# A hand-written engine order through the RG-LRU rounds, with a two-phase long convolution as filler

## The chip, the cores and the metric

The kernel runs on one core of a Trainium2 chip. A core has five engines, each with its own in-order instruction queue: TensorE (PE in the profile) multiplies matrices and writes to PSUM, VectorE (DVE) and ScalarE (ACT) read and write both memories, GpSimd (POOL) works on SBUF alone, and SyncE (SP) issues most of the transfers. [...]

The metric is the device time of one execution in microseconds. Three runs of the kernel before gave 1373.71, 1376.23 and 1376.35 us; the median is 1376.23 us.

## What is computed

Two layers over a latent stream `x` of 1024 tokens with 1024 channels, with 256 context tokens beside it. The even layer is where the change lies (shapes for one sample, float32 throughout):

```python
z = h @ p["w_in"]                              # h: modulated rmsnorm of x
va, vg, ga, xb, gb = split(z)                  # 1024 channels each
u   = va * sigmoid(vg)                         # branch A
u   = depthwise_conv(u, conv_w, conv_b)        # 31 taps
y_a = silu(layernorm(u)) * silu(ga)
u   = depthwise_conv(xb, sconv_w, sconv_b)     # branch B: 4 taps
r, i = sigmoid(u @ w_r + b_r), sigmoid(u @ w_i + b_i)     # per head of 128, both directions
a   = exp(-8 * r * softplus(-lam))
bx  = sqrt(1 - a*a) * (i * u)
y_b = scan_forward(a, bx) + scan_backward(a, bx)          # started from the state after the context
y_b = y_b * silu(gb)
x   = x + gate * (concat([y_a, y_b]) @ p["w_out"])
```

The odd layer (a pooling mixer with two large products) and a last RMSNorm follow; nothing in them is changed.

## The kernel before

Tokens lie along the free dimension, channels along the 128 partitions, so each 1024-channel tensor is eight tiles of 128x1024. Products are made in three passes of a float32 split into a high and a low part (`mm3_steps`, lines 121 to 129: high x high, high x low, low x high), which is 24 matmuls of 512 columns for half a tile. A weight tile is loaded into a ring of two raw tiles (`wr`), its high part is cast on ScalarE into a ring of two (`wh`) and its low part is subtracted on POOL into a ring of two (`wl`); `wload` and `split` do this (lines 94 to 118).

The stages that matter here, with the names by which the profile shows them:

- Start: modulation, RMSNorm, and the first two of four weight foldings (to line 428). It leaves `hh`, `hl` (the latent stream in two parts) and `ch`, `cl` (the context).
- Recurrence (lines 430 to 586), a round for each tile `j`. The projections of a round are xb (latent tokens, into the two-bank PSUM tile `xb`) and xbc (context), vg and va, and four gates `g` (two directions, two gates each, in pieces of 256, 512 and 512 columns). The short convolution makes `uc` (first tap on ScalarE, line 531; three on VectorE, line 534), which is split into `uh` and `ul` for the gates' products. `u = va * sigmoid(vg)` (line 564) is the input of branch A. Of the previous tile, ScalarE makes tanh, exp and root (`decays`), POOL two products for each direction (lines 463 and 465), VectorE a combination and two scans for each direction (lines 468, 475, 477) and the sum of the directions (line 480), which goes to HBM (`yb_raw`).
- gb (lines 717 to 730): for each tile the projection gb, its SiLU, the product with `yb_raw` (read back as `yr`), and the split into `ybh`, `ybl`.
- The long convolution (lines 734 to 768): for each tile one start on ScalarE and 30 taps of about 1013 columns on VectorE, accumulating in the two-bank PSUM tile `conv`; sums over tiles for the mean go to `lnsum`, on POOL for tiles 1 to 5. It depends on `u` alone, so the scheduler spreads it over the recurrence, gb and wob stages.
- LayerNorm (lines 771 to 785): the mean by a product with a matrix of equal entries (`mu`), 16 subtractions (line 776), squares on ScalarE (lines 778, 781), their sums on VectorE for the first half of the tokens and on POOL for the second (line 783), a product `ms_ln`, a root and a reciprocal for each half; then 16 products (line 823) and a SiLU for each tile (line 824).
- wob (lines 788 to 798): the product of branch B's half of `w_out` with `ybh`, `ybl`; VectorE adds it to `x` out of PSUM (line 796).
- ga (lines 830 to 853): the projection ga, its SiLU in place in PSUM, the product with `u` (line 838), and the splits for the next product.

Matmul outputs of one bank come from a ring of four PSUM banks (`pm`); two further tiles of two banks each (`cv`, `xb`) serve the convolution and the projection xb. Two tile rings of SBUF hold the recurrence's tiles (`ltile`, six of 128x1280; `utile`, four), and four half tiles (`ttile`) serve the sigmoids.

The order on each engine is set by the scheduler of the framework, which places instructions by an estimated timeline and by the priority of the program order; `tc.high_priority` moves an instruction ahead, and `tc.issue_after` places one behind another. Once compiled, the order is fixed. In the recurrence of the kernel before, `issue_after` ties only ScalarE's decays to one another and a few instructions to them. Of the gate weights it says

```python
gws = wload(gw[j], f"gw{j}", nc.gpsimd, n=4 * P)
weave(gate_steps(j, gws, (uh, ul), gates), steps, 2)
```

so their high and low parts take a place in the rings `wh` and `wl` among xb, vg and va.

## Time and profile before

| | |
|---|---|
| median of the runs shown | 1376.23 us |
| the profiled execution itself | 1381.07 us |
| its span, first to last instruction | 1379.3 us |
| TensorE busy, mean granted clock | 1295.9 us (94%), 0.974 |
| VectorE busy | 1205.1 us (87%) |
| ScalarE, POOL busy | 632.7 us (46%), 363.3 us (26%) |
| recurrence, first vg matmul to first gb matmul | 104.3 to 476.4 us |
| gb, wob, ga | to 570.3, 663.4, 750.7 us |

A row of a view by stages has the stage, its length, and for PE, the weight load, DVE, ACT and POOL the busy time with the number of instructions in brackets; then the granted clock of TensorE (1.00 is full), the share of the transfer engines and GB/s. A row of a timeline has the start, the duration of the row's instructions (xN of them together), engine, line, operation and operands; in square brackets the idle time ahead of it and who ended it. A group's row has the count, busy time and mean in ns of one, and the idle time. A row of a tile's view has the shortest, median and longest duration in ns. The execution profiled is a single one, so times read from it are compared with its own 1381.07 us.

### The profile page before, as it was taken

The page shows a single profiled execution, that of the slowest core. Times are in us where ns is not written, and L with a number is a line of the kernel's source. Part 1 is how long each engine was busy: PE and PEld are TensorE (multiplying, and loading weights), DVE is VectorE, ACT ScalarE, POOL GpSimd, SP SyncE. Part 2 cuts the span into 40 slices and gives each one's busy share as a digit, 9 for nine tenths or more (in the row PEclk, how much of TensorE's full clock was granted, in tenths as well). Part 3 has the DMA queues.
Part 4 walks back from the last instruction along what each step waited for, and adds up shares of the span by engine and source line. Part 5 has one row for each costly group of instructions (what it writes and reads, how often), then busy time and mean ns, then how long its engine had stood idle before and what let it go on. Part 6 is the DMA issues. An engine that isn't in the chain of part 4 may idle for free.

```text
span 1379.3 us, 15637 instructions
## 1 busy us (share of the span) xinstructions
PE 1295.9 (94%) x5664; PEld 1048.2 (76%) x5664; DVE 1205.1 (87%) x1587; ACT 632.7 (46%) x906; POOL 363.3 (26%) x182
## 2 busy tenths in 40 slices
PE   7889989898999799999998999999999999999896
PEld 4468868787777587787887887788888888778685
DVE  7998999999999999998778865999999987876775
ACT  6353644674465542304533544754334344634442
POOL 5173534743473555523320004000000000000002
PEclk9899999999999899999999999999999999999997
DMA  9753011111112113343353646424243334758623
GB/s 354 280 180 119 25 59 54 53 40 61 54 35 72 46 46 130 110 151 135 103 185 122 221 154 205 138 93 151 100 145 123 115 115 132 265 190 275 206 107 123
DMA packets 82866, 181.79 MB, mean 132 GB/s; under 512 B 7778, under 2 KB 27618, under 8 KB 82788
## 3 DMA queue, kind: packets, MB, share of 16 engines
q1 hardware_dynamic: 74340, 176.60, 37.8%
q10 hardware_dynamic: 8448, 4.20, 1.0%
q8 instruction: 44, 0.72, 0.2%
q14 instruction: 34, 0.28, 0.1%
HBM read 136.72 MB, written 44.04 MB: 131 GB/s over the span
## 4 chain that ended last, share of the span: by engine, by line
PE 36%; DVE 10%; DMA 7%; issue 2%; ACT 2%; POOL 1%; POOLq 0%; SPq 0%; DVEq 0%; ACTq 0%
PE ga L127 2%; PE ga L128 2%; PE ga L126 2%; PE wob L127 2%; PE wob L128 2%; PE wob L126 2%; DMA wr_g<-wg 1%; DVE ws L986 1%; DMA yr_t<-y_t 1%; DMA wr_v<-wfold 1%; PE qb_g L666 1%; DVE wq_g L96 1%; PE qb_g L669 1%; PE qb_g L668 1%; DVE wq_wo L96 1%
## 5 line engine op out<-in xcount | busy, mean ns | idle before, releaser
L746 DVE SCALAR_TENSOR_TENSOR conv<-u,sm,conv 128x1013 f32<-128x1013 f32 (+14 forms) x232 | 291.2, 1272 | 6.6 <-ACT conv L738 3.8
L1252 POOL TENSOR_TENSOR o<-x,rr 128x256 f32<-128x256 f32 (+1 forms) x9 | 8.0, 923 | 462.9 <-ACT rr L1240 460.0
L511 ACT ACTIVATE g<-g,sm 128x512 f32<-128x512 f32 (+1 forms) x96 | 58.8, 617 | 110.5 <-PE g L510 108.3
L96 POOL TENSOR_TENSOR wl_wu<-wr_wu,wh_wu 128x1024 fp32r<-128x1024 f32 x16 | 39.4, 2470 | 153.9 <-ACT wh_wu L95 147.7
L463 POOL TENSOR_TENSOR g<-g,uc 128x1280 f32<-128x1280 f32 x16 | 47.5, 2967 | 107.9 <-ACT g L511 65.1
L249 PE MATMUL fold<-gh,wh_wu 128*128 128x512 f32 x128 | 53.0, 416 | 5.7 <-ACT wh_wu L95 5.7
L250 PE MATMUL fold<-gl,wh_wu 128*128 128x512 f32 x128 | 52.4, 409 | 3.2 <-DVE gl L96 3.2
L128 PE MATMUL gb<-h0h,wl_gb 128*128 128x512 f32 x128 | 50.7, 398 | 4.8 <-POOL wl_gb L96 4.8
L126 PE MATMUL vg<-h0h,wh_vg 128*128 128x512 f32 x128 | 52.3, 408 | 2.7 <-ACT g L511 2.1
L251 PE MATMUL fold<-gh,wl_wu 128*128 128x512 f32 x128 | 50.7, 405 | 2.3 <-POOL wl_wu L96 2.3
L128 PE MATMUL xb<-h0h,wl_xb 128*128 128x512 f32 x128 | 50.2, 392 | 2.0 <-POOL wl_xb L96 2.0
L127 PE MATMUL wob<-ybl,wh_wob 128*128 128x512 f32 x128 | 50.5, 395 | 1.2 <-POOL ybl L96 1.2
L465 POOL TENSOR_TENSOR g<-g,th 128x1280 f32<-128x1280 f32 x16 | 46.9, 2948 | 16.8 <-ACT th L449 16.8
L127 PE MATMUL vg<-h0l,wh_vg 128*128 128x512 f32 x128 | 51.2, 400 | 0.0
L126 PE MATMUL gb<-h0h,wh_gb 128*128 128x512 f32 x128 | 50.6, 395 | 0.1
L126 PE MATMUL va<-h0h,wh_va 128*128 128x512 f32 x128 | 50.6, 395 | 0.0
L127 PE MATMUL va<-h0l,wh_va 128*128 128x512 f32 x128 | 50.6, 395 | 0.0
L508 PE MATMUL g<-uh,wh_gw 128*128 128x512 f32 (+1 forms) x96 | 36.3, 379 | 15.1 <-ACT wh_gw L95 6.4
L126 PE MATMUL wob<-ybh,wh_wob 128*128 128x512 f32 x128 | 50.6, 396 | 0.0
L128 PE MATMUL wob<-ybh,wl_wob 128*128 128x512 f32 x128 | 49.9, 391 | 0.7 <-POOL wl_wob L96 0.7
L128 PE MATMUL va<-h0h,wl_va 128*128 128x512 f32 x128 | 50.4, 395 | 0.0
L127 PE MATMUL gb<-h0l,wh_gb 128*128 128x512 f32 x128 | 50.4, 393 | 0.0
(548 smaller groups left out, 4301.1 us busy)
## 6 DMA issues: line engine op xcount, KB each, us to landing
mod<-modT SPq DMA_DIRECT2D x28, 512.0 KB, 5.5
wr_wu<-wu SPq DMA_DIRECT2D x16, 512.0 KB, 3.9
x_part<-xp SPq DMA_DIRECT2D x32, 256.0 KB, 2.4
mod<-modT SPq DMA_DIRECT2D x32, 256.0 KB, 3.3
wr_v<-wfold SPq DMA_DIRECT2D x16, 512.0 KB, 3.7
wr_g<-wg SPq DMA_DIRECT2D x16, 512.0 KB, 5.4
wr_wo<-wo SPq DMA_DIRECT2D x16, 512.0 KB, 4.2
yr_t<-y_t SPq DMA_DIRECT2D x16, 512.0 KB, 6.3
```

The lines of the kernel that those rows point to most:

```text
L96: eng.tensor_tensor(out=lo, in0=src, in1=hi.bitcast(F32), op=sub))
L126: nc.tensor.matmul(ps, hi[:, kc], xh[k][:, cols], start=(k == 0), stop=False)
L127: nc.tensor.matmul(ps, hi[:, kc], xl[k][:, cols], start=False, stop=False)
L128: nc.tensor.matmul(ps, lo[:, kc], xh[k][:, cols], start=False, stop=(k == ks - 1))
L249: nc.tensor.matmul(ps, wh[:, kc], gh[i], start=(i == 0), stop=False)
L250: nc.tensor.matmul(ps, wh[:, kc], gl[i], start=False, stop=False)
L251: nc.tensor.matmul(ps, wl[:, kc], gh[i], start=False, stop=(i == 3))
L463: nc.gpsimd.tensor_tensor(out=ius[d], in0=ius[d], in1=uc, op=mult)
L465: nc.gpsimd.tensor_tensor(out=ius[d], in0=ius[d], in1=roots[d], op=mult)
L508: nc.tensor.matmul(ps[:, :n], gwh[:, kc], uh[:, a : a + n], start=True, stop=False)
L511: nc.scalar.activation(t[:, a : a + n], ps[:, :n], AF.Sigmoid, bias=col(ob + d * KT + j))
L746: nc.vector.scalar_tensor_tensor(out=(us[j] if k == 30 else acp)[:, a:b], in0=us[j][:, a + o : b + o], scalar=col(O_CONVW + 31 * j + k), i ...
```

## The change

Three things are changed, all in the even layer, and what is computed stays the same.

1. From the recurrence to the end of gb, every instruction of TensorE, VectorE, ScalarE and POOL is placed behind the one written ahead of it (`on`, with one last instruction for each engine), so each engine's order is that of the program text. A round is written out anew: its projections, the previous tile's tanh, exp, root, scans, and the casts and low parts of the weights, loaded by `raw_load` and split by `raw_split`. xbc and its taps now come ahead of xb; xb of the next tile is woven into the gates, 16 steps of three matmuls over 12 gate pieces. In the last round gb0 takes xb's place. gb runs two tiles ahead of the product with `yb_raw`, and the weights of the first two wob tiles are cast there too. Six fixed tiles `L` replace the ring `ltile`, and the modulation's tiles for the gate go through them ahead of round 0.
2. The long convolution works on even and odd tokens apart (`conv`): two convolutions of 15 and 16 taps on the halves with every second tap, one of 16 on the sum of the halves with summed weights (`wsum`, the last weight alone), and recombinations. Its instructions have some 508 columns and read every second element of `u`; both accumulators lie in the one PSUM tile. Each instruction is a step, and `fill(n)` takes the next n steps at a fixed place in VectorE's order: 32 in a round, 22 behind the last round, 6 for each half tile of gb. What is left at the end of gb (62 of 414 steps) is placed by the scheduler as before. All `lnsum` additions are on VectorE.
3. The gate weights' high and low parts move from the weights' rings to the half tiles of `tpool`.

```diff
+    def on(eng, f, *args, **kw):
+        with ExitStack() as octx:
+            if eng in last:
+                octx.enter_context(tc.issue_after(last[eng].ins))
+            last[eng] = f(*args, **kw)
+        return last[eng]
...
+    def raw_split(raw, name):
+        hi = wpool.tile([P, D], F32R, tag="wh", name=f"wh_{name}")
+        lo = wpool.tile([P, D], F32R, tag="wl", name=f"wl_{name}")
+        cast(hi, raw)
+        gp(out=lo, in0=raw, in1=hi.bitcast(F32), op=sub)
+        return hi, lo
...
+    def tap(acc_, src, w, o, last_=False):
+        a, b = max(0, -o), H - max(0, o)
+        vec(nc.vector.scalar_tensor_tensor, out=(src if last_ else acc_)[:, a:b], in0=src[:, a + o : b + o],
+            scalar=w, in1=acc_[:, a:b], op0=mult, op1=add)
+        if last_:
+            vec(nc.vector.tensor_copy, out=src[:, b:], in_=acc_[:, b:])
+
+    def conv(j, n):
+        acp = wide(f"conv{j}", n)
+        ue, uo = us[j][:, 0::2], us[j][:, 1::2]
+        acc_, late, bias = acp[:, HALF[0]], acp[:, HALF[1]], col(O_CONVB + j)
...
+        for n in range(NT + 1):
+            if n < NT - 1 and n != 7:
+                tap(acc_, ue, w(2 * n + 1), n - 7)
+                yield
+            if n != 8:
+                tap(late, uo, w(2 * n), n - 8)
+                yield
...
+        vec(nc.vector.tensor_tensor, out=uo, in0=uo, in1=ue, op=add)
+        yield
...
+        for n in range(NT + 1):
+            if n != 7:
+                tap(acc_, uo, wsum[:, j, n : n + 1] if n < NT else w(30), n - 7, n == NT)
+                yield
...
         for j in range(KT):
+            vg = [psum(f"vg{j}_{h}") for h in range(2)]
+            all_of(mm3_fixed(vg[0], w, (hh, hl), HALF[0]))
+            if state is not None:
+                rec_input(state, 1)
+            fill(2)
+            first_tap(j, xb, uc[:, C:])
+            other_taps(j, xb, uc[:, C:], 1)
+            if state is not None:
+                rec_tanh(state)
+            wva = raw_split(raw_load(win[j], f"va{j}"), f"va{j}")
+            if state is not None:
+                rec_exp(state)
             uh, ul = utile(f"uh{j}", F32R), utile(f"ul{j}", F32R)
+            cast(uh, uc)
+            all_of(mm3_fixed(vg[1], w, (hh, hl), HALF[1]))
+            fill(4)
+            vec(nc.vector.tensor_tensor, out=ul, in0=uc, in1=uh.bitcast(F32), op=sub)
+            if state is not None:
+                rec_root(state)
+                rec_scaled(state, 0)
+            name = "gb0" if final else f"xb{j + 1}"
+            wnext = raw_split(raw_load(win[4 * KT] if final else win[3 * KT + j + 1], name), name)
+            gwh, gwl = [tpool.tile([P, H], F32R, tag="t", name=f"w{n}_gw{j}") for n in "hl"]
+            raw = wpool.tile([P, H], F32, tag="wr", name=f"wr_gw{j}")
+            nc.sync.dma_start(raw, gw[j])
+            cast(gwh, raw)
+            gp(out=gwl, in0=raw, in1=gwh.bitcast(F32), op=sub)
+            if state is not None:
+                rec_scaled(state, 1)
...
+            for h in range(2):
+                ps = psum(f"va{j}_{h}")
+                all_of(mm3_fixed(ps, wva, (hh, hl), HALF[h]))
+                fill((8, 5)[h])
+                vec(nc.vector.tensor_tensor, out=u[:, HALF[h]], in0=ps, in1=sg[h], op=mult)
...
+            if state is not None:
+                rec_scan(state, 0)
+            if not final:
+                other_taps(j + 1, xc, ucn[:, :C])
+            if state is not None:
+                rec_scan(state, 1)
+                rec_sum(state)
...
+            for n, _ in enumerate(gate_steps(j, (gwh, gwl), (uh, ul), gates)):
+                while done < 16 * (n + 1) // 12:
+                    next(steps)
+                    done += 1
+                if n == 5:
+                    rec_input(now, 0)
+                if n == 6:
+                    w = raw_split(raw, name)
+            all_of(steps)
+            fill(10)
...
     for j in range(KT):
+        if j > 0:
+            sbs[j] = [ttile(f"sb{j}_{h}") for h in range(2)]
+            for h in range(2):
+                act(sbs[j][h], gps[j][h], AF.Silu)
+        if j + 2 < KT:
+            gps[j + 2] = [psum(f"gb{j + 2}_{h}") for h in range(2)]
+            for h in range(2):
+                all_of(mm3_fixed(gps[j + 2][h], gws[j + 2], (hh, hl), HALF[h]))
         th, tl = d2tile(f"ybh{j}", F32R), d2tile(f"ybl{j}", F32R)
         for h in range(2):
             y = vtile(f"yr{j}_{h}")
             nc.sync.dma_start(y, yb_raw[j][:, HALF[h]])
+            vec(nc.vector.tensor_tensor, out=y, in0=y, in1=sbs[j][h], op=mult)
+            cast(th[:, HALF[h]], y)
+            gp(out=tl[:, HALF[h]], in0=y, in1=th[:, HALF[h]].bitcast(F32), op=sub)
+            fill(6)
+        gb_weights(j + 3)
...
+    fixed[0] = False
+    all_of(going[0])
+    for j in range(begun[0], KT, 2):
+        all_of(zip(*[conv(k, n) for n, k in enumerate(range(j, min(j + 2, KT)))]))
```

329 lines of the change are left out of this document (177 added, 152 removed).

## The prediction

> **What bounds the kernel now.** I read the busy times of the page first, then the busy times by stage (recurrence, gb, wob, ga, cut at their first matmuls), then the groups of VectorE, then single stretches of the timeline.
>
> ```profile
> span 1379.3 us, 15637 instructions
> PE 1295.9 (94%) x5664; PEld 1048.2 (76%) x5664; DVE 1205.1 (87%) x1587; ACT 632.7 (46%) x906; POOL 363.3 (26%) x182
> ...
> 104.30:476.40 372.10, 345.40 (x1586) 284.15 (x1584) 353.49 (x297) 203.26 (x238) 176.38 (x69) 0.96 0.16 54
> 476.40:570.30 93.90, 89.12 (x384) 73.02 (x385) 92.28 (x77) 38.12 (x48) 54.23 (x29) 0.98 0.29 96
> 570.30:663.40 93.10, 91.25 (x393) 73.40 (x392) 86.69 (x94) 23.21 (x32) 34.43 (x19) 1.00 0.42 142
> 663.40:750.70 87.30, 87.30 (x385) 72.15 (x384) 67.11 (x145) 35.72 (x49) 17.26 (x7) 1.00 0.45 146
> ...
> 465.27 0.28 PE L508 MATMUL g<-uh,wh_gw 128*128 128x256 f32 x1
> 465.39 0.28 PE L509 MATMUL g<-ul,wh_gw 128*128 128x256 f32 x1
> ```
>
> The ga stage is TensorE at its pace: 385 matmuls in 87.30 us, 0.227 us each; 256 columns take 0.12 (465.27 to 465.39). By these the recurrence needs 7 rounds of 168 x 0.227 + 36 x 0.12 = 42.4 us, a last one of 28.7 and 2.9 for the first xbc: 328.4 of its 372.1 us. gb needs 87.1 of 93.9, wob 87.1 of 93.1. So 56.5 us are TensorE's idle or slow time. VectorE is busy 95% of the recurrence and 98% of gb: it sets both stages.
>
> ```profile
> L468 DVE SCALAR_TENSOR_TENSOR g<-g,g 128x1280 f32<-128x1280 f32 x16 | 42.4, 2650 | 5.9 <-POOL g L465 5.9
> ...
> L468 DVE SCALAR_TENSOR_TENSOR g<-g,g x16: 1458/2511/4243, 164.6 to 499.4; 128x1280 f32<-128x1280 f32 x16
> L475 DVE TENSOR_TENSOR_SCAN g<-g,g x16: 657/680/2875, 169.9 to 507.1; 128x256 f32<-128x256 f32 x16
> L477 DVE TENSOR_TENSOR_SCAN g<-g,g x16: 2320/2336/4480, 176.6 to 512.3; 128x1024 f32<-128x1024 f32 x16
> ...
> 259.55 3.85 DVE L468 SCALAR_TENSOR_TENSOR g<-g,g 128x1280 f32<-128x1280 f32 x1
> ...
> 259.09 2.96 POOL L465 TENSOR_TENSOR g<-g,th 128x1280 f32<-128x1280 f32 x1
> ```
>
> The first row gives a mean of 2.65 us for an instruction whose shortest is 1.458: 42.4 - 16 x 1.458 = 19 us, 2.4 a round, are lost in this line alone, and the two scans below it also reach 2.9 and 4.5 us at their longest. The pair at 259 shows the occasion: the drawn-out one of 3.85 us starts inside an instruction of POOL. All of them have two inputs in SBUF. The taps (one input in PSUM) show none of this.
>
> **The change part by part.** *Long convolution.* What a VectorE instruction costs in a queue is the step to the next one, not its duration, since neighbours overlap by some 0.08 us:
>
> ```profile
> 584.26 0.74 DVE L796 SCALAR_TENSOR_TENSOR xp<-wob,m,xp 128x512 f32<-128x512 f32 x1
> 584.93 4.81 DVE L746 SCALAR_TENSOR_TENSOR conv<-u,sm,conv 128x1015 f32<-128x1015 f32 x4
> 589.65 0.74 DVE L796 SCALAR_TENSOR_TENSOR xp<-wob,m,xp 128x512 f32<-128x512 f32 x1
> ```
>
> Four full taps take 589.65 - 584.93 = 4.72 us, 1.18 each; a 512-column instruction with a PSUM operand takes 584.93 - 584.26 = 0.667. Before, a channel tile is 30 x 1.18 = 35.4 us. After, it is 49 PSUM instructions of about 508 columns (2 starts, 28 + 1 taps, 2 recombinations, 15 taps, 1 finish), 49 x 0.667 = 32.7, and some 1.2 us of small ones and one sum: 33.9. That is 12 us less over eight tiles; lnsum additions moved from POOL to VectorE (ten of 0.6 us) give 6 back. The two phases alone are worth 6 us of VectorE, nothing on TensorE. All of this takes a read of every second word as free, which no row shows: a half-tap lies between 0.667 (the 512-column row) and 1.18 us (as if all words between were read). I take 0.667, the row with the same count of elements.
>
> *The order of a round.* Let T be the end of xb on TensorE. Rows for the round:
>
> ```profile
> 243.26 1.20 ACT L531 ACTIVATE uc<-xb,sm 128x1024 f32<-128x1024 f32 x1
> 244.70 2.62 ACT L449 ACTIVATE th<-g,chalf 128x1280 f32<-128x1280 f32 x2
> 247.78 1.05 ACT L95 CAST wh_va<-wr_va 128x1024 fp32r<-128x1024 f32 x1
> 249.44 1.28 ACT L449 ACT_TABLE_LOAD   x1
> 258.59 0.60 ACT L552 ACTIVATE sg<-vg 128x512 f32<-128x512 f32 x1
> 291.71 1.20 ACT L531 ACTIVATE uc<-xb,sm 128x1024 f32<-128x1024 f32 x1
> ...
> 272.97 0.68 DVE L564 TENSOR_TENSOR u<-va,sg 128x512 f32<-128x512 f32 x1
> 273.57 1.48 DVE L571 TENSOR_TENSOR ul<-uc,uh 128x1280 fp32r<-128x1280 f32 x1
> 248.29 1.28 DVE L534 SCALAR_TENSOR_TENSOR uc<-xb,sm,uc 128x1022 f32<-128x1022 f32 x1
> 287.26 0.48 DVE L534 SCALAR_TENSOR_TENSOR uc<-xbc,sm,uc 128x255 f32<-128x255 f32 x1
> 280.75 1.21 DVE L480 TENSOR_TENSOR g<-g,g 128x1024 f32<-128x1024 f32 x1
> ...
> 286.04 2.96 POOL L463 TENSOR_TENSOR g<-g,uc 128x1280 f32<-128x1280 f32 x1 [13.04 <-PE g L510]
> 291.31 2.40 POOL L96 TENSOR_TENSOR wl_vg<-wr_vg,wh_vg 128x1024 fp32r<-128x1024 f32 x1 [2.30 <-ACT wh_vg L95]
> ```
>
> Before, a round is 291.71 - 243.26 = 48.45 us (from one first tap on xb to the next). After, VectorE has in a round: 32 conv steps 21.3, three long and three short taps 4.8, ul 1.4, two u 1.2, two scan groups of 4.2, a sum 1.1: 38.2 us, and waits 1.4 for the first tap behind T. That fits in TensorE's 42.4. Now the timetable by these rows, each engine in its written order, all times behind T. VectorE's taps and fills end at 9.6. ScalarE (first tap, tanh, va cast, load, exp, uh cast, load) has uh at 10.2, the first root at 12.8, sg at 17.6 and 18.1. VectorE goes on with ul (11.6), eight fills (16.9), u0 (18.3), u1 (22.6, since va's second half ends at 21.8), scans (26.8), ctx taps (28.0), scans (32.2), sum (33.4), ten fills (40.1) and two of the next round. POOL ends its first input at 2.3, va lo 7.4, scaled input 15.8, xb lo 18.2, gate lo 19.5, second scaled input 22.5, and begins the next input at 33.5, when half of the gates are there. So POOL is idle while VectorE runs its two-SBUF-input instructions, by 0.1 us at both ends, and TensorE waits for nobody: its weights are there 3 us ahead, and the bank of its fourth gate matmul (needed at 29.1) is read out by the ctx taps at 28.0. SP's order of the loads is unchanged but for the gate weights, whose cast no longer waits for va's matmuls since their tiles left that ring; yb_raw is stored once a round as before. I take 42.8 a round and 2 us in round 0, where eight mod sums stand ahead of ul: 328.4 + 10.9 (gb0 in the last round) + 4.8 = 344.1, so gb1 begins at 448.4, against gb at 476.4.
>
> *gb, by hand.* Rows:
>
> ```profile
> 526.30 0.68 DVE L727 TENSOR_TENSOR yr<-yr,sb 128x512 f32<-128x512 f32 x1
> 526.90 1.26 DVE L746 SCALAR_TENSOR_TENSOR conv<-u,sm,conv 128x1015 f32<-128x1015 f32 x1
> ...
> 454.43 0.58 PE L508 MATMUL g<-uh,wh_gw 128*128 128x256 f32 x1 [6.44 <-ACT wh_gw L95]
> ...
> 456.08 0.63 PE L126 MATMUL va<-h0h,wh_va 128*128 128x512 f32 x1
> ...
> 460.78 0.39 PE L126 MATMUL va<-h0h,wh_va 128*128 128x512 f32 x1
> ```
>
> gb1 and gb2 are done 21.8 us after that. gb3's weight cast stands on ScalarE behind y's second cast, and that behind VectorE's 22 fills (14.7), scans held by POOL to 16.9 (25.3), sum 26.5, y 27.1, six fills 31.1, y 31.7, casts 33.4; POOL's lo 35.8. TensorE idles 13.6 us, then runs slowly as at 456.08 to 460.78 (11 matmuls in 4.70 us, 2.2 us lost). Later tiles: VectorE's loop 9.3 us against 10.9, no wait. 76.2 + 15.8 = 92.0: wob begins at 540.4. There the two first tiles are woven together, so both weight slots come free late and the third tile's lo part is about 3.5 us late: 90.6, wob ends at 631.0, 32.4 us early.
>
> *LayerNorm and ga.* This part is not ordered by hand, but its place moves. In the compiled order of before, the mean is taken in wob's sixth tile; after, all wob evictions but the last stand ahead of it on VectorE, the mean's matmul in wob's last half.
>
> ```profile
> 631.50 9.66 DVE L776 TENSOR_TENSOR u<-u,mu 128x512 f32<-128x512 f32 x16 [1.60 <-PE mu L773]
> 655.70 3.35 DVE L184 RECIPROCAL lnsum<-sq_ln 128x512 f32<-128x512 f32 x1 [3.53 <-ACT sq_ln L183]
> 659.54 4.90 DVE L823 TENSOR_TENSOR u<-u,lnsum 128x512 f32<-128x512 f32 x8
> 665.02 3.34 DVE L184 RECIPROCAL lnsum<-sq_ln 128x512 f32<-128x512 f32 x1
> 673.22 0.68 DVE L838 TENSOR_TENSOR u<-u,ga 128x512 f32<-128x512 f32 x1
> ```
>
> Before, the first ga product comes 673.22 - 663.40 = 9.8 us into ga, and four PSUM banks (4 x 5.44 us) cover it. After, with W the end of wob: subtractions to W+7.9; ScalarE's squares alternate with ga casts and SiLUs that wait for TensorE (W+10.9, W+16.3), first root at W+20.4, reciprocal 23.8, products 28.6, reciprocal 32.0, products 36.8, first ga product W+37.5. TensorE stops at W+22.6 and goes on at W+37.6: 15 us, and 2.2 us of slow clock. ga ends at 631.0 + 87.1 + 17.2 = 735.3, against 750.7. Behind it nothing is changed: -15.4 us.
>
> **Sum.** Against the profiled execution, 1381.07 us: 1365.7. The median of the runs shown, 1376.23, is 0.35% below that execution, so 1361. Bounds: the holes in gb and ga between 0 and 20 us each, a round between 42.4 and 48.45.
>
> **Rivals.** *The gain passes through.* If the LayerNorm keeps up (its chain is the longest that I add up by hand) the 32.4 us stay: (1381.07 - 32.4) x 0.9965 = 1344. For it: ScalarE is only 41% busy there. Against: the compiled order. *Strided reads cost (slower).* Place: every fill step. With half the span of the bounds, +0.26 us, a round is 38.2 + 8.3 + 1.4 = 47.9, gb1 begins at 486, its tail, loops and rest take 30 + 99 + 68, so the convolution ends at 683; the LayerNorm's 44 us (629 to 673) and 12 ga halves (65) end ga at 792: +41, 1417; with the whole span 1520. It decides from about +0.15 us a step. Nothing in the rows speaks for or against, since every large access is contiguous. [...] *POOL's hold on VectorE stays (slower).* The margins are 0.1 us; two holds of 2.96 a round less the slack of 2.8 is 3.1 x 7 = 22 us, leaving +7: 1383. It decides from 2.2 us a round. For it: what the recurrence loses to it now. Against: the order above. *No change*: the holes eat all.
>
> **Chances.** Forecast 0.50 (1350 to 1371), gain passes through 0.17, no change 0.05, POOL's hold 0.18, strided reads 0.10. Faster by over 0.2% (about what a measurement can tell from no change) 0.67, same 0.05, slower 0.28. The range 1340 to 1395 leaves out the strided case and tails.
>
> **What would show it.** First taps (ACT, uc<-xb) 42.5 to 43.5 us apart; half-taps stepping by 0.66; scan groups near 1.46, 0.66 and 2.32 us; one idle stretch of TensorE of 10 to 15 us in front of gb's fourth tile waiting for its weights, another in the third ga tile waiting for VectorE. Wrong if half-taps take 0.9 or more, if rounds stay above 45, or if ga shows no hole.

## The result and the profile after

| | before | after |
|---|---|---|
| median of four runs | 1376.29 us (1373.71 to 1377.03) | 1414.26 us (1409.65 to 1421.14) |
| ratio | | 1.0283, 95% interval 1.0239 to 1.0328 |
| span of the profiled execution, granted clock | 1379.3 us, 0.974 | 1412.0 us, 0.962 |

The change makes the kernel 2.8% slower; 1361 us and "faster" were forecast. From the page of the changed kernel, the span and the busy times:

```profile
span 1412.0 us, 15817 instructions
PE 1295.2 (92%) x5664; PEld 1051.2 (74%) x5664; DVE 1215.2 (86%) x1790; ACT 628.3 (44%) x900; POOL 349.0 (25%) x172
```

TensorE has the same work in a longer span. VectorE has 10 us more instead of less. By stages (to the end of the last gates with gb0 among them, gb1 to gb7, wob, ga):

```profile
104.30:481.70 377.40, 351.80 (x1627) 294.60 (x1626) 344.90 (x388) 199.70 (x231) 176.32 (x64) 0.96 0.17 60
481.70:586.90 105.20, 81.17 (x343) 66.13 (x342) 101.74 (x138) 35.31 (x46) 41.58 (x23) 0.87 0.22 79
586.90:677.90 91.00, 89.29 (x389) 72.58 (x388) 77.36 (x118) 13.18 (x17) 23.96 (x12) 1.00 0.41 144
677.90:786.30 108.40, 92.20 (x391) 74.76 (x390) 85.27 (x171) 48.04 (x67) 26.16 (x14) 0.92 0.35 117
```

gb1 begins at 481.7 (forecast 448.4), wob 105.2 us later (92.0), ga 91.0 later (90.6), and ga takes 108.4 (104.3). So 33 us of the 51 by which ga ends late come from the rounds, 13 from gb, 4 from ga; behind ga nothing differs by more than 3 us. Two of the changed kernel's first taps on xb, from ScalarE's timeline, show a round:

```profile
245.62 1.20 ACT L437 ACTIVATE uc<-xb,sm 128x1024 f32<-128x1024 f32 x1
293.82 1.21 ACT L437 ACTIVATE uc<-xb,sm 128x1024 f32<-128x1024 f32 x1 [0.67 <-PE xb L437]
```

This one takes 48.2 us. The seven are 45.8, 42.5, 45.3, 48.2, 45.6, 48.4 and 49.7, 46.5 in the mean, where 42.8 was forecast. The 48.45 that the prediction read before is one round of seven; the kernel before has 43.2 to 49.7, 47.2 in the mean, so the hand-written order shortened a round by 0.7 us and not by 5.6. The chain of half-taps behind the last round, from VectorE's timeline in the changed kernel:

```profile
495.91 10.98 DVE L437 SCALAR_TENSOR_TENSOR conv<-u,wsum,conv 128x505 f32<-128x505 f32 x14
```

A chain of full taps from the same view of the kernel before, which the prediction did not show:

```profile
620.79 5.20 DVE L746 SCALAR_TENSOR_TENSOR conv<-u,sm,conv 128x1013 f32<-128x1013 f32 x4
```

The group of the changed kernel's first-phase half-taps, from its page:

```profile
L437 DVE SCALAR_TENSOR_TENSOR conv<-u,sm,conv 128x505 f32<-128x505 f32 (+6 forms) x196 | 147.1, 751 | 5.8
```

A half-tap lasts 0.75, as the 512-column row of the prediction does, so stepping over every second word costs nothing here. But fourteen of them step by (10.98 - 0.75) / 13 = 0.787, not 0.667. The four full taps step by (5.20 - 1.27) / 3 = 1.31, where the four that the prediction quoted step by 1.18. The two kinds differ in what they wait for. In the quoted four, taps of two tiles alternate; in these four, and in the fourteen, each instruction waits for the one directly ahead. Start to start, the steps from tap to tap in the trace of before fall into two clusters: 77 of 1.30 to 1.33 us (median 1.315) and 45 of about 1.18. In the changed kernel there is one: 283 steps from half-tap to half-tap have a median of 0.787 (0.767 to 0.82), and one of 2.9 is left out. The trace shows that these instructions wait for VectorE's own semaphore, not for which instruction; that they wait for the one directly ahead follows from the program. The half-taps of the first phase do so although they alternate between two accumulators: both halves lie in one PSUM tile, and the waits are kept by tile. The run e1 tests this.

In the changed kernel's timeline around the end of a round, VectorE against POOL:

```profile
283.78 5.68 DVE L437 TENSOR_TENSOR_SCAN l<-l,l 128x256 f32<-128x256 f32 x2
284.36 2.96 POOL L437 TENSOR_TENSOR l<-l,uc 128x1280 f32<-128x1280 f32 x1 [9.87 <-PE g L437]
287.26 4.41 POOL L437 TENSOR_TENSOR wl_vg<-wr_vg,wh_vg 128x1024 fp32r<-128x1024 f32 x1
289.50 3.25 DVE L437 TENSOR_TENSOR l<-l,l 128x1024 f32<-128x1024 f32 x1
```

POOL's next input begins 38.7 us behind the first tap at 245.62, as soon as half of the gates are there, but VectorE is still in its last scans (the forecast had the sum done at T + 33.4, the input at 33.5): the two scans take 5.68 instead of the 3.08 of a round without this overlap, the sum 3.25 instead of 1.23 (both shown below, from the run e4). The waits of TensorE up to the end of ga have two large rows (us in total, times, longest):

```profile
PE gb L437 <- ACT sb L437: 23.0, 1, 23.0
PE ga L126 <- DVE u L982: 14.7, 1, 14.7
```

The first of them in the timeline, the idle time ahead of each row and its releaser in brackets:

```profile
518.96 0.69 DVE L437 TENSOR_TENSOR yr<-yr,sb 128x512 f32<-128x512 f32 x1
519.68 0.62 ACT L437 CAST ybh<-yr 128x512 fp32r<-128x512 f32 x1 [20.90 <-DVE yr L437]
528.01 0.80 PE L437 MATMUL gb<-h0h,wh_gb 128*128 128x512 f32 x1 [23.03 <-ACT sb L437]
```

y0 comes late on VectorE, ScalarE stands behind it with gb1's SiLU and gb3's cast, and TensorE waits for both.

### The profile page after: what moved, and what is told of

It reads as the page before. It is cut to its first block, busy times and chain, and to the rows that moved or that the text cites. A ratio compares the mean times of both kernels' runs of the same rounds, so it can differ in the third digit from the quotient of the medians.

```text
span 1412.0 us, 15817 instructions
## 1 busy us (share of the span) xinstructions
PE 1295.2 (92%) x5664; PEld 1051.2 (74%) x5664; DVE 1215.2 (86%) x1790; ACT 628.3 (44%) x900; POOL 349.0 (25%) x172
## 4 chain that ended last, share of the span: by engine, by line
PE 39%; DVE 26%; DMA 8%; issue 3%; ACT 2%; POOL 2%; POOLq 0%; DVEq 0%; SPq 0%; ACTq 0%
DVE conv L437 7%; DVE l L437 6%; PE gb L437 4%; PE wob L128 2%; PE wob L126 2%; PE wob L127 2%; PE ga L126 2%; PE ga L127 2%; PE ga L128 2%; DVE u L437 2%; DVE uc L437 1%; DMA yr_t<-y_t 1%; DMA wr_wu<-wu 1%; PE qb_g L837 1%; PE qb_g L840 1%
## 5 line engine op out<-in xcount | busy, mean ns | idle before, releaser
L437 DVE SCALAR_TENSOR_TENSOR conv<-u,sm,conv 128x505 f32<-128x505 f32 (+6 forms) x196 | 147.1, 751 | 5.8
L437 ACT ACTIVATE l<-g,sm 128x512 f32<-128x512 f32 (+1 forms) x96 | 58.8, 618 | 83.0 <-PE g L437 60.5
L437 POOL TENSOR_TENSOR l<-l,uc 128x1280 f32<-128x1280 f32 x16 | 50.3, 3144 | 98.7 <-PE g L437 71.6
L437 POOL TENSOR_TENSOR l<-l,l 128x1280 f32<-128x1280 f32 x16 | 54.1, 3383 | 72.2 <-ACT l L437 72.2
L437 DVE SCALAR_TENSOR_TENSOR conv<-u,wsum,conv 128x505 f32<-128x505 f32 (+6 forms) x92 | 69.0, 750 | 2.7
L437 DVE TENSOR_TENSOR_SCAN l<-l,l 128x256 f32<-128x256 f32 (+1 forms) x32 | 64.2, 2006 | 1.1
L126 PE MATMUL ga<-h0h,wh_ga 128*128 128x512 f32 x128 | 51.0, 398 | 14.7 <-DVE u L982 14.7
L128 PE MATMUL ga<-h0h,wl_ga 128*128 128x512 f32 x128 | 51.2, 400 | 0.0
L128 PE MATMUL wob<-ybh,wl_wob 128*128 128x512 f32 x128 | 49.7, 393 | 1.3 <-POOL wl_wob L96 1.3
L127 PE MATMUL ga<-h0l,wh_ga 128*128 128x512 f32 x128 | 50.8, 397 | 0.0
L126 PE MATMUL wob<-ybh,wh_wob 128*128 128x512 f32 x128 | 49.7, 393 | 0.5 <-ACT wh_wob L95 0.5
L437 PE MATMUL vg<-h0h,wl_vg 128*128 128x512 f32 x128 | 49.8, 389 | 0.0
```

The costliest lines, as they stand in the source:

```text
L126: nc.tensor.matmul(ps, hi[:, kc], xh[k][:, cols], start=(k == 0), stop=False)
L127: nc.tensor.matmul(ps, hi[:, kc], xl[k][:, cols], start=False, stop=False)
L128: nc.tensor.matmul(ps, lo[:, kc], xh[k][:, cols], start=False, stop=(k == ks - 1))
L437: last[eng] = f(*args, **kw)
```

## The experiments

The theory after the result: an instruction of VectorE that waits for the one directly ahead costs 0.12 to 0.13 us more (A). Rivals: the half-taps' strided reads (B), POOL's hold on scans and sums (C), and, for the holes in gb and ga, that each is a loss of its own. Each ratio is to the kernel before on the same chip. The chips differ, and there the kernel before took 1374.6 to 1379.5 us, so differences between the medians of two rows are rough: by the ratios most runs come out up to 4 us better against the changed kernel than by the medians. "Conv ends" is the end of the convolution's last instruction in the trace, "rest" the span of that execution less this.

| run | median us | ratio, 95% | gb1 begins | conv ends | rest |
|---|---|---|---|---|---|
| before | 1376.3 | | 476.4 (gb0) | 628.0 | 751.3 |
| after | 1414.3 | 1.0283 (1.0239 to 1.0328) | 481.7 | 668.8 | 743.3 |
| e1_halves | 1396.4 | 1.0132 (1.0098 to 1.0166) | 471.7 | 646.7 | 745.7 |
| e2_gb | 1412.2 | 1.0244 (1.0209 to 1.028) | 479.1 | 663.1 | 743.3 |
| e3_mods | 1414.5 | 1.0259 (1.0224 to 1.0294) | | 667.2 | 747.1 |
| e4_fills | 1418.7 | 1.0293 (1.0259 to 1.0326) | 449.8 | 675.0 | 740.3 |
| a1_onephase | 1412.2 | 1.0259 (1.0225 to 1.0294) | 468.0 | 667.9 | 741.4 |
| b1_gw | 1403.1 | 1.0194 (1.016 to 1.0228) | | 644.0 | 753.2 |
| b2_two | 1395.5 | 1.0145 (1.0109 to 1.0181) | | 608.7 | 784.9 |
| e7_all28 | 1397.8 | 1.0166 (1.0134 to 1.0199) | 454.1 | 651.9 | 743.9 |
| x1_nochain | 1382.2 | 1.0032 (1.0012 to 1.0052) | | 635.4 | 747.9 |
| x2_leave28 | 1395.5 | 1.0126 (1.0102 to 1.0149) | | 639.8 | 754.1 |
| x3_mods | 1408.9 | 1.0214 (1.0178 to 1.0249) | | 659.4 | 749.5 |
| x4_best | 1384.3 | 1.0048 (1.0024 to 1.0072) | | 642.5 | 743.4 |
| y0_swap | 1409.5 | 1.0229 (1.0185 to 1.0274) | | 661.0 | 746.7 |
| y1_swap28 | 1380.4 | 1.0022 (1.0007 to 1.0037) | | 639.1 | 740.3 |
| y2_swap30 | 1372.5 | 0.9974 (0.9949 to 1.0) | | 634.0 | 746.8 |
| x5_nochain28 | 1373.5 | 0.997 (0.9952 to 0.9989) | | 632.0 | 738.1 |
| z1_wob30 | 1370.2 | 0.9932 (0.992 to 0.9945) | | 615.9 | 752.5 |
| z2_wob28 | 1373.4 | 0.9957 (0.9944 to 0.9971) | | 624.7 | 746.9 |

The last two columns are of the one execution that was profiled. The last is nearly constant, 738 to 750 us, over all kernels in the hand-written order except two (754 and 752), however early TensorE comes to gb1. This suggests that the end of the convolution on VectorE sets the time; x2 and x1 below test it by taking work out of the convolution.

**The price of waiting: the halves as two tiles.**

```diff
     def wide(name, n):
-        return pc.tile([P, S], F32, tag=("cv", "xb")[n % 2], name=name)
+        if n % 2 == 0:
+            return Pair([pc.tile([P, H], F32, tag=f"cv{h}", name=f"{name}_{h}") for h in range(2)])
+        return pc.tile([P, S], F32, tag="xb", name=name)
...
```

`Pair` passes a slice on to the tile that holds it.

> The changed kernel with one thing altered: the two halves of the convolution's accumulator are two PSUM tiles instead of two halves of one, so that 196 of the 313 half-taps that wait for the VectorE instruction directly ahead of them wait for an older one. Theory A (an instruction that waits for the one directly ahead steps by its duration and 0.035 us, 0.787, and one that doesn't by 0.667): half-taps of the first phase step by 0.667, 49 steps a tile lose 24 x 0.12 = 2.9 us, a round goes from 46.6 to about 44, the time from 1414 to about 1390. Theory B (half-taps are slow by themselves, by their strided reads): the step stays 0.787, the time 1414 within 4. Theory C (what the rounds lose is POOL's hold on VectorE): the step falls to 0.667 but rounds stay above 45.5 and the time above 1403.

From VectorE's timeline of this run, a chain of the second phase and one of the first:

```profile
199.68 7.06 DVE L449 SCALAR_TENSOR_TENSOR conv<-u,wsum,conv 128x506 f32<-128x506 f32 x9
...
217.57 4.65 DVE L449 SCALAR_TENSOR_TENSOR conv<-u,sm,conv 128x505 f32<-128x505 f32 x7
```

The second row steps by (4.65 - 0.75) / 6 = 0.65; the first, a true chain on one accumulator, still by 0.79. In the whole trace 162 steps now have a median of 0.653 and 121 one of 0.786. Nothing else about these instructions changed, so A is shown and B is out. The time falls by 18 us, to 1396, where 1390 was expected: the rounds fall only from 46.5 to 45.9 in the mean, so C is not out beside A.

**One phase in place of two.** The convolution as 31 full taps a tile, 0.6 of one for each step of `fill`; the fills, the order and all else as changed.

> The changed kernel with the convolution in its old one-phase form (31 full taps a tile, each 1.27 us) as the fill, 0.6 full taps for each half-tap, everything else as changed. Theory A: of 240 taps 171 wait for the instruction directly ahead and step by 1.31, 69 by 1.18, which with the starts is 316 us of VectorE against 322 for the two-phase form: 1408 within 6, so the two phases bring nothing. Theory B (the half-taps' strided reads are the loss): 1385 or less.

1412 us, the changed kernel's time within the noise, and the convolution ends within 1 us of the same moment. B would have given 1385. Full taps that chain cost 1.315 each (169 steps from tap to tap, all between 1.30 and 1.33), half-taps that chain 0.787 each, and by either form a tile is 40 us. So, chained, the two phases bring nothing.

**Fewer steps in a round.**

```diff
-                fill((8, 5)[h])
+                fill((6, 3)[h])
...
-            fill(10)
+            fill(4)
```

> The changed kernel with 22 convolution steps a round instead of 32 (8 and 5 become 6 and 3, 10 becomes 4), the other ten left for gb and later. If VectorE's work sets the round (Theory A): rounds of 42.5 to 43.5 us instead of 46.6, and the 70 steps, 55 us of VectorE, come back in gb, wob or ahead of ga: the time between 1390 (half of it beside TensorE) and 1420. If the order or POOL's hold sets it (Theory C): rounds stay above 45, time 1420 or more.

First taps on xb, and the end of a round, from this run's timeline:

```profile
241.80 1.21 ACT L437 ACTIVATE uc<-xb,sm 128x1024 f32<-128x1024 f32 x1 [0.67 <-PE xb L437]
284.28 1.21 ACT L437 ACTIVATE uc<-xb,sm 128x1024 f32<-128x1024 f32 x1 [0.67 <-PE xb L437]
...
271.68 3.08 DVE L437 TENSOR_TENSOR_SCAN l<-l,l 128x256 f32<-128x256 f32 x2
274.79 1.23 DVE L437 TENSOR_TENSOR l<-l,l 128x1024 f32<-128x1024 f32 x1
274.82 4.02 POOL L437 TENSOR_TENSOR l<-l,uc 128x1280 f32<-128x1280 f32 x1 [10.96 <-PE g L437]
```

With 22 steps each round behind round 0 is 42.5 us, as A had it, and gb1 begins at 449.8, the forecast's 448.4 within 1.4. The timetable of VectorE and POOL is nearly right, but not to its margin of 0.1 us: the sum runs from T + 33.0 to T + 34.3, where it was to be done at 33.4, and POOL's input begins at T + 33.1, where 33.5 was forecast. So the two overlap even here. The sum is ahead by 0.03 us, and now POOL is the one drawn out, 4.02 instead of 2.96. In the fourth round behind round 0 POOL's input is ahead, by 0.07 us, and the sum takes 3.97 instead of 1.23. In both it is the one that starts second that is drawn out; so it is in the prediction's pair at 259, where POOL's product is 0.46 us ahead and takes 2.96, and VectorE's takes 3.85 instead of 1.46. Yet the kernel is no faster, 1419: VectorE was done no earlier (the convolution ends at 675.0 instead of 668.8), since the 70 steps stand in gb and later. 32 us gained at gb1 were worth nothing.

**The tail ahead of gb3, and round 0.** In the first run SiLU of gb1, gb2's matmuls and gb3's weights stand ahead of the 20 fills; in the second the eight mod sums stand behind round 0's value products in the text.

```diff
+        gps[2] = [psum(f"gb2_{h}") for h in range(2)]
+        for h in range(2):
+            all_of(mm3_fixed(gps[2][h], gws[2], (hh, hl), HALF[h]))
+        sbs[1] = [ttile(f"sb1_{h}") for h in range(2)]
+        for h in range(2):
+            act(sbs[1][h], gps[1][h], AF.Silu)
+        gb_weights(3)
         fill(20)
...
```

> The changed kernel with the tail of the recurrence reordered: SiLU of gb1, the matmuls of gb2 and the weight split of gb3 stand ahead of the 20 fills and of y's first product, everything in gb one iteration earlier. If TensorE's 23 us ahead of gb3 are a loss of their own, wob begins about 20 us earlier and the time is 1390 to 1396. Rival: VectorE is full from the recurrence to the LayerNorm, so its end sets ga: wob begins earlier by 20 us, the hole in ga grows by as much from 14.7, and the time stays above 1408.

> The changed kernel with the eight gate modulation sums of round 0 moved from ahead of the round to behind its value products, where they stood before. In the changed kernel VectorE waits 12.7 us for their loads ahead of them and round 0 loses 8 us on TensorE. If that is passed on: 1406 to 1409. If VectorE's later work swallows it: 1412 to 1416.

From the waits of TensorE in the first of them:

```profile
PE ga L126 <- DVE u L989: 14.7, 1, 14.7
PE gb L437 <- ACT sb L437: 12.1, 1, 12.1
```

The hole ahead of gb3 shrinks from 23.0 to 12.1 and wob begins at 573.2 instead of 586.9, but wob then takes 8 us more (it waits for y's casts), and its end and ga's come only 5.7 us earlier, as the convolution's does; the median is 2 us lower. That is the rival's outcome, though the gain went into wob and not into ga's hole. The second has the time of the changed kernel and says nothing on round 0. Only the text moved: VectorE still waits 12.7 us for the mods' loads there, since those sums are not in the hand-written chain.

**The parts on the kernel before.** Gate weights through the half tiles alone, then the two phases alone (with the halves as two tiles), in the compiled order:

```diff
-            gws = wload(gw[j], f"gw{j}", nc.gpsimd, n=4 * P) if last else None
+            gws = wload(gw[j], f"gw{j}", nc.gpsimd, n=4 * P, out=gw_tile) if last else None
...
```

> The kernel before with one part of the change alone: the gate weights' split goes to the ring of 512-column tiles instead of the weights' ring. If VectorE's work up to the LayerNorm sets the end, as the runs so far say: 1376 within 4. If TensorE's waits for these weights (6.4 us in the last round) counted: 1365 to 1370.

> The kernel before with the two-phase convolution alone, in the compiled order, its accumulator in two PSUM tiles so that 99 steps wait for the one directly ahead and the rest don't. Theory A: 99 x 0.787 and 293 x 0.66 and 12 us of small ones is 283 us against 296 for the old form, less 5 for additions that come to VectorE: the LayerNorm begins 8 us earlier, 1368 to 1374. Theory B: 1385 or more.

The first misses both of its ranges. The second lies in B's (1385 or more), but not for B's reason, as its convolution ends early. TensorE's waits in the recurrence of the first:

```profile
PE va L128 <- POOL wl_va L96: 21.9, 5, 4.7
PE g L511 <- ACT uh L541: 16.2, 1, 16.2
```

With the gate weights out of the ring the compiled order is another one: POOL's low part of va comes up to 4.7 us late in five rounds, and uh 16.2 us late in the last. These are 38 us of waits that the kernel before does not have, for a part that looked free; what in the order moved them stays open. In the second, the convolution ends at 608.7, 19 us ahead of the kernel before, where A had 8, yet it is 1.4% slower: rounds of up to 56.7 us, in which TensorE's gates wait 14.1 us in all for ul on VectorE, against 6.7 before. Here TensorE sets the end: wob ends 15 us later than in the kernel before, and the span is 14 us longer; hence the 785 in the last column. So neither part is faster by itself in the compiled order.

**Work taken from VectorE, and the forecast's price made true.** One run leaves out 28 steps; the other has the halves as two tiles and lays the second phase in turn on both, so that nearly no step waits for the one ahead. Neither gives the convolution's sums; they are for the time alone:

```diff
-            if n != 7:
+            if n != 7 and (j < KT - 2 or n == NT):
                 tap(acc_, uo, wsum[:, j, n : n + 1] if n < NT else w(30), n - 7, n == NT)
```

```diff
-                tap(acc_, uo, wsum[:, j, n : n + 1] if n < NT else w(30), n - 7, n == NT)
+                tap(late if n % 2 else acc_, uo, wsum[:, j, n : n + 1] if n < NT else w(30), n - 7, n == NT)
```

> The changed kernel without the 14 second-phase taps of each of the last two tiles: 28 steps x 0.787 = 22 us of VectorE left out of the convolution, nothing else. If VectorE's work up to the LayerNorm sets the end: 1390 to 1395, and the 14.7 us hole in ga shrinks to nothing. If TensorE's own way through gb and wob sets it: 1405 or more.

> The changed kernel with the accumulator's halves as two tiles, and the second phase's 15 taps laid in turn on the one half and the other, so that 36 steps instead of 313 wait for the instruction directly ahead (the sums are then not the convolution's: the cost alone is of interest). This is the price the forecast assumed, 0.66 a step. If that price was the whole error of the forecast: 1355 to 1370. If VectorE's work up to the LayerNorm sets the end, 80 steps x 0.13 = 10 us less than with the two tiles alone (1396): 1383 to 1388, and what is missing to the forecast lies elsewhere (round 0, POOL's hold, the tail).

22 us of VectorE left out give 18.8 us, and ga's hole of 14.7 us is gone from TensorE's waits: VectorE's sum is the bound, until TensorE becomes it. With the price that the forecast assumed for nearly every half-tap the kernel takes 1382: 32 of the 53 us of the error (35 by the ratios) are the wait for the instruction directly ahead, some 20 are not. The rounds still are 42.5 to 48.8 us in that run, and POOL's hold is still there. VectorE's scans, first products and sums in it:

```profile
L449 DVE TENSOR_TENSOR_SCAN l<-l,l 128x256 f32<-128x256 f32 (+1 forms) x32 | 66.2, 2068 | 1.1
L449 DVE SCALAR_TENSOR_TENSOR l<-l,l 128x1280 f32<-128x1280 f32 x16 | 23.6, 1478 | 0.0
L449 DVE TENSOR_TENSOR l<-l,l 128x1024 f32<-128x1024 f32 x8 | 22.5, 2809 | 0.3
```

They take 112.3 us together, no less than in the changed kernel (110.2, shown further below).

**Round 0 for good, and the edits together.**

```diff
+            if j == 0:
+                for m in range(2 * KT, 3 * KT):
+                    raw = L[m % 6][:, :D]
+                    nc.sync.dma_start(raw, modT[0, m])
+                    v = m0[:, 0, m : m + 1]
+                    vec(nc.vector.scalar_tensor_tensor, out=raw, in0=raw, scalar=1.0, in1=cL, op0=mult, op1=mult,
+                        accum_out=v)
+                    vec(nc.vector.tensor_tensor, out=v, in0=v, in1=col(O_MB + m), op=add)
```

> The changed kernel with the eight modulation sums of round 0 in VectorE's written order behind the value products (in the run before that tried this the scheduler had left them where they were). The first taps on xb then start about 9 us earlier and the sums fill VectorE's waits of 4.8 and 7.6 us in round 0. If VectorE's work sets the end: 1403 to 1408. If not: 1412 to 1416.

> The changed kernel with four edits together: the accumulator's halves as two PSUM tiles, 28 convolution steps a round instead of 32, the mod sums of round 0 back behind its value products, and the tail of the recurrence reordered as in the run before. If VectorE's work sets the end: rounds of 42.5, scans and sums free of POOL's hold (20 us less on VectorE than with the halves alone), the convolution ends at 620 to 630 instead of 647, TensorE waits over 25 us in ga for it, and the time is 1365 to 1380. If what the halves left is TensorE's holes: 1350 to 1360. If nothing adds up: 1390.

> The run with four edits (two tiles, 28 steps a round, tail reordered; 1398) with the modulation sums written behind the value products and the LayerNorm's sums of tiles on POOL instead of VectorE. VectorE is rid of about 9 us of waiting and 8 to 10 us of sums: 1378 to 1384 if both come off the path; 1388 or more if POOL's sums hold VectorE up.

The sums written into VectorE's chain bring 5.4 us (9.5 by the ratios), to 1408.9, where 1403 to 1408 was expected: the convolution ends 9.4 us earlier, and round 0 is 37.7 us instead of 45.8. The four edits together gave 1398, not 1365 to 1380: TensorE is through wob at 640, 38 us earlier than in the changed kernel, and waits 30 us behind it, because the convolution ends at 652. One of the four was the edit without effect (e3). With it made good and the sums of tiles on POOL (x4) the time is 1384, the upper end of what was expected.

**POOL's order.**

```diff
-                if n == 5:
-                    rec_input(now, 0)
                 if n == 6:
                     w = raw_split(raw, name)
+                    rec_input(now, 0)
```

> The changed kernel with two neighbours of POOL's written order exchanged: the low part of vg's weights ahead of the next recurrence's first input, so that POOL's first two-input instruction of the round begins about 2 us later behind T. If POOL's hold on the last scans and the sum (4.6 us a round in the changed kernel) depends on that moment and 2 us are enough: rounds of 44 instead of 46.6, scans and sums 20 us shorter, 1390 to 1397. If VectorE is late by more than that anyhow, since its round is 43.5 us without any hold: rounds stay above 45.5, 1405 to 1416.

> The run with two tiles, 28 steps a round and the tail reordered (1398), with the modulation sums behind the value products (about 5 us, as the run of that edit alone) and POOL's two neighbours exchanged. If the hold goes, VectorE has 20 to 25 us less work up to the LayerNorm: 1366 to 1376. If it stays: 1388 to 1394.

> As the run beside it with 30 convolution steps a round, and the LayerNorm's sums of tiles on POOL from the end of the hand-written part on. If VectorE's work alone sets the end and the timetable holds: 1362 to 1374, at most 4 us off the run beside it, since the steps are only moved. If 30 steps break the timetable: 1385 or more.

> The run with 28 steps, tail, modulation sums and POOL's exchange, with the second phase laid in turn on the two halves (not the convolution's sums), so that nearly no step waits for the one directly ahead: all that the forecast assumed, at once. If half-tap price, POOL's hold, round 0 and the tail are the whole of the forecast's error: 1352 to 1366. If something else is missing: 1372 or more.

By itself (y0) the exchange keeps the first three rounds behind round 0 at 42.5 to 43.4; the next are 48.9, 48.1 and 50.9, 1409.5 in all: VectorE, with 32 chained steps, falls behind by more than the 2 us. With 28 steps, two tiles, the new tail and the sums of round 0 made good (y1) the time is 1380.4, short of the 1366 to 1376 expected: the rounds are 42.5 to 44.4, but the convolution ends only at 639. With 30 steps, and part of the sums of tiles on POOL (y2), every round behind round 0 is 42.5, and the time is 1372.5, as expected. The end of a round, from that run's timeline:

```profile
309.80 1.23 DVE L449 TENSOR_TENSOR l<-l,l 128x1024 f32<-128x1024 f32 x1
310.94 7.42 DVE L449 SCALAR_TENSOR_TENSOR conv<-u,sm,conv 128x510 f32<-128x510 f32 x11
312.27 2.41 POOL L449 TENSOR_TENSOR wl_vg<-wr_vg,wh_vg 128x1024 fp32r<-128x1024 f32 x1 [12.95 <-ACT wh_vg L449]
```

The sum ends at 311.03, and POOL begins 1.2 us behind it. The run that comes nearest to all of the forecast's assumptions at once (x5; its price of a half-tap, hardly any hold and a round 0 without the loss, though with 28 steps a round; again without the convolution's sums) still takes 1373.5, above the 1366 that would have closed the account. The waits of TensorE in it:

```profile
PE ga L137 <- DVE u L1003: 12.7, 1, 12.7
PE ms_ln L192 <- DVE lnsum L948: 9.9, 1, 9.9
PE ms_ln L192 <- POOL lnsum L948: 4.4, 1, 4.4
```

wob is done at 622, ahead of the forecast's 631, but the convolution at 632; the LayerNorm's chain costs TensorE 27 us instead of the forecast's 15.

**wob's evictions off VectorE.** ScalarE scales, POOL adds, and wob stands ahead of the LayerNorm in the text:

```diff
-                nc.vector.scalar_tensor_tensor(out=t, in0=ps, scalar=m0[:, 0, 2 * KT + m : 2 * KT + m + 1],
-                                               in1=t, op0=mult, op1=add)
+                s = ttile(f"xs{m}_{h}")
+                nc.scalar.activation(s, ps, AF.Identity, scale=m0[:, 0, 2 * KT + m : 2 * KT + m + 1])
+                nc.gpsimd.tensor_tensor(out=t, in0=t, in1=s, op=add)
```

> The run with 30 steps and POOL's exchange (1372.5) with wob's evictions taken from VectorE: ScalarE scales the PSUM bank, POOL adds, and they stand ahead of the LayerNorm in the program. VectorE is rid of 15 x 0.66 = 10 us ahead of the LayerNorm. If VectorE's work up to the LayerNorm still sets the end: 1361 to 1366. If ScalarE's or POOL's new work stands in the LayerNorm's or TensorE's way: 1372 or more.

> The same with 28 convolution steps a round instead of 30: TensorE's wait ahead of gb3 is shorter (5 us instead of 12), the LayerNorm's start the same, so within 4 us of the run beside it if VectorE sets the end, and 5 to 8 us below it if TensorE does by now.

The first of the two by stages, cut as for the changed kernel:

```profile
104.30:444.60 340.30, 338.46 (x1626) 285.22 (x1625) 311.08 (x375) 200.43 (x232) 162.51 (x64) 1.00 0.20 66
444.60:536.00 91.40, 80.95 (x345) 66.06 (x344) 89.81 (x128) 33.34 (x43) 42.87 (x22) 0.93 0.28 91
536.00:628.20 92.20, 89.81 (x386) 72.75 (x385) 79.60 (x119) 21.95 (x31) 48.96 (x30) 0.98 0.44 144
628.20:738.70 110.50, 93.82 (x393) 75.24 (x392) 90.81 (x174) 50.38 (x70) 28.65 (x15) 0.91 0.35 115
```

The first subtraction of the mean in its timeline:

```profile
629.06 9.66 DVE L955 TENSOR_TENSOR u<-u,mu 128x512 f32<-128x512 f32 x16 [11.73 <-PE mu L952]
```

1370.2 us, 0.68% below the kernel before (interval 0.55% to 0.80%), is the fastest of all, and lies between the two outcomes that were expected. The convolution now ends at 616, 18 us earlier than in y2's profiled execution, but the mean's matmul stands behind wob on TensorE, and VectorE waits 11.7 us for it: the bound has moved to the compiled order of the LayerNorm. So the 18 us are not passed on whole: 12 between the two profiled executions, about 6 by the ratios. The stages are nearly the forecast's: wob ends at 628.2 (631.0), ga at 738.7 (735.3). With 28 steps (z2) the time is 1373.4, 3 us above this run, within the 4 us that were expected if VectorE sets the end.

## Why the prediction was wrong

**The step of the half-tap (the first term that failed).** "49 PSUM instructions ... 49 x 0.667": the row behind it is an instruction followed by an independent one. 283 of the steps in the trace are chained and measured 0.787. A tile is 40 us instead of 33.9, against 35.4 in the forecast's sum for before; start to start the convolution costs VectorE 322 us after and 296 before, so it grew by 26 us where 12 less were forecast. The 1.18 for a full tap had the same flaw, and only 77 of the steps in before pay for it. The wait is worth 32 us of the time (x1). A row for it stood in the trace of before, 620.79; the prediction read the one at 584.93.

**The strided reads.** Taken as free, with a rival at 1417 us. They are free in these instructions: 0.75 us with either access (0.751 in the mean of 196 half-taps, 0.74 for the 512-column row of the prediction). That the result lies next to 1417 is chance; the surplus of a chained step is there with contiguous full taps too (1.315 in a1, against 1.18 for the taps that alternate in the kernel before).

**The order of a round (the second that failed).** The length of a round was right where VectorE is on time (e4: rounds of 42.5, gb1 at 449.8). "So POOL is idle while VectorE runs its two-SBUF-input instructions, by 0.1 us at both ends" was not: even in e4 the sum and POOL's input overlap by 1.2 us. The fills were also counted as equal, 0.667 each. In the changed kernel's first round behind round 0 the step between the two phases of the first tile, several instructions long, falls among the five fills ahead of u1, which take 5.6 us instead of 3.3. From VectorE's timeline:

```profile
176.01 2.31 DVE L437 SCALAR_TENSOR_TENSOR conv<-u,sm,conv 128x507 f32<-128x507 f32 x3
178.23 1.76 DVE L437 SCALAR_TENSOR_TENSOR edge_junk<-u,sm 128x8 f32<-128x8 f32 x1
...
181.62 0.69 DVE L437 TENSOR_TENSOR u<-va,sg 128x512 f32<-128x512 f32 x1
...
192.78 3.80 DVE L437 TENSOR_TENSOR l<-l,l 128x1024 f32<-128x1024 f32 x1
```

VectorE is then 1.9 us behind e4 (the sum begins at T + 34.9 instead of 33.0), POOL's input goes first, the sum takes 3.80 instead of 1.23, and the next round begins later still; two rounds on, at 283.78, the scans and the sum lose 4.6 us. What it costs, from VectorE's groups of scans, first products and sums in the changed kernel:

```profile
L437 DVE TENSOR_TENSOR_SCAN l<-l,l 128x256 f32<-128x256 f32 (+1 forms) x32 | 64.2, 2006 | 1.1
L437 DVE SCALAR_TENSOR_TENSOR l<-l,l 128x1280 f32<-128x1280 f32 x16 | 31.6, 1977 | 0.0
L437 DVE TENSOR_TENSOR l<-l,l 128x1024 f32<-128x1024 f32 x8 | 14.4, 1799 | 0.3
```

The same groups in z1, where the rounds keep time:

```profile
L449 DVE TENSOR_TENSOR_SCAN l<-l,l 128x256 f32<-128x256 f32 (+1 forms) x32 | 48.7, 1521 | 1.1
L449 DVE SCALAR_TENSOR_TENSOR l<-l,l 128x1280 f32<-128x1280 f32 x16 | 24.3, 1520 | 0.0
L449 DVE TENSOR_TENSOR l<-l,l 128x1024 f32<-128x1024 f32 x8 | 11.8, 1478 | 0.3
```

110.2 - 84.8 = 25.4 us of VectorE, 3.6 a round. In the kernel before the same groups take 111.8 us, so the hand-written order of the change removed next to nothing of the hold that it was to remove. That is the rival "POOL's hold on VectorE stays", which had 22 us and a threshold of 2.2 a round. It happened beside the first error and not because of it: x1, with the forecast's price, is as late in that round (its sum takes 3.79) and has 112.3 us in these groups.

**Round 0.** 2 us were allowed. VectorE waited for the mods' loads:

```profile
113.04 1.23 DVE L212 SCALAR_TENSOR_TENSOR l<-l,cL 128x1024 f32<-128x1024 f32 x1 [12.70 <-DMA l<-modT]
```

Round 0 took 45.8 instead of the 37.7 of x3; the time lost to it was 5 us (9.5 by the ratios).

**gb.** The hole ahead of gb3 was foreseen with its mechanism, 13.6 us; it is 23.0, since VectorE came to y0 late. It cost little (e2), because it lies beside VectorE's work.

**The LayerNorm and ga (the path that failed).** "TensorE stops at W+22.6 and goes on at W+37.6" was right in mechanism and size: a hole of 14.7 us, where 15 were forecast, about 3 us later behind W, with W itself 47 us later. What it missed is whose end sets W and the mean: the prediction counted VectorE for a round and for gb, but never added its work up to the mean. It took TensorE's wob as the frame and the convolution as done in time. All hand-ordered runs but two show the convolution's end plus 738 to 750 us. In x5, where wob ends 9 us ahead of the forecast, the convolution ends 10 us behind wob, TensorE's holes there are 27 us instead of 15, and ga takes 122 us instead of 104; its profiled execution takes 1371.9 us against 1365.7. In z1, where VectorE's convolution is no longer late, the time is 4.5 us above the forecast for a profiled execution (1370.2 against 1365.7). The other half of z1's difference to 1361 is the 0.35% between the profiled execution and the median of before, which was carried over to a kernel that need not have it. What part of it is real stays open.

**The gate weights' ring.** Costed at nothing, with more room for their cast. In the hand-written order nothing speaks against that, though no run takes this part out of it; in the compiled order the same edit alone costs 1.9%.

## What to carry to other kernels

Price an instruction by its step in the dependency that it will have: on VectorE a chain on one accumulator, or on two halves of one tile, paid 0.13 us an instruction more than an alternation between two tiles (0.787 against 0.653 in e1). Add up the whole work of the busiest engine to the point where the next stage needs it before adding up rounds; filling another engine's holes gives nothing while that sum stands. A hand-written order with 0.1 us to spare between two instructions that hold each other up is not on time (in e4 POOL's input began 0.03 us behind VectorE's sum and took 4.02 us instead of 2.96): leave it 1 to 2 us, as the exchange of two POOL instructions did (1.2 us in y2), and place steps that are longer than the rest by their own cost.

## What the runs showed of the hardware

- On VectorE, the step from start to start was longer where an instruction waits for the one directly ahead: 0.787 against 0.653 us at 508 columns, 1.315 against 1.18 at 1015, so 0.13 us at either length (scalar_tensor_tensor with one input in PSUM; the changed kernel, e1 and the kernel before).
- Reading every second 4-byte word of an SBUF row cost nothing in these instructions, one input of which is in PSUM: 0.751 us in the mean for 196 half-taps, 0.74 to 0.75 for contiguous rows of 512 columns.
- An instruction of VectorE with two inputs in SBUF and one of POOL held each other up, in both directions: POOL's 2.96 us input took 4.02 when VectorE's sum of 1.23 us was 0.03 us ahead of it (e4), and the sum took 3.25 to 3.97 when POOL's instruction was ahead (3.25 in the rows of the changed kernel, 3.97 in one round of e4).
